# Seven products for the convolutions' half of an output projection, sums made on the output tiles, and an opening with its work put in another order

## The chip, the cores and the metric

The kernel runs on one core of a Trainium2 chip. A core has five engines with their own instruction queues: TensorE (PE, matmuls into PSUM), VectorE (DVE), ScalarE (ACT), GpSimd (POOL) and SyncE (SP), whose queue issues all the transfers here. The metric is the device time of one execution in microseconds, the median of several. All arithmetic is in float32. TensorE multiplies float32 operands in a form that keeps only the leading part of each (`fp32r`), so an operand is split into a high part (a copy on ScalarE that rounds) and a low part (a subtraction on VectorE), and a product is made of three matmuls: high by high, high by low, low by high.

## The reference

One decoder layer over a sequence of 2048 positions of 1024 features:

```python
h = rmsnorm(x, norm1_g)
p_q, p_k, p_v, p_g, p_a, c_b, c_c, c_h = split(h @ w_in)      # 256 256 512 512 16 512 512 512
o_gla = rmsnorm(gla(q, k, v, log_a)) * silu(p_g)              # gated linear attention, 4 heads of 128
o_conv = c_b * causal_depthwise_conv(c_c * c_h, conv_w)       # width 3 over positions, 512 features
x = x + concatenate([o_gla, o_conv]) @ w_out                  # 512 + 512 features -> 1024
h2 = rmsnorm(x, norm2_g)
x = x + (silu(h2 @ w_ffn_gate) * (h2 @ w_ffn_up)) @ w_ffn_down    # 1024 -> 2816 -> 1024
return rmsnorm(x, norm_f_g)
```

## The kernel before

Activations lie with features on the 128 partitions and positions along the free dimension: a tile is 128 features by 512 positions. The 2048 positions are four blocks of 512 and two halves of two blocks each. A half goes through a stage as one matrix of two block columns.

Most products are made with Strassen's scheme in Winograd's form, in *units*: a unit takes a weight matrix as four quarters (A11, A12, A21, A22) and an operand as four quarters (rows of features by the two blocks: B11, B12, B21, B22), and makes the 2 x 2 output tiles in seven products instead of eight. The list `PRODUCTS` pairs the weights A11, S1, S2, A12, S3, S4, A22 with the operands B11, T1, T2, B21, T3, B22, T4. The S are sums and differences of weight quarters, made on GpSimd in `unit_weights`; the T are differences of operand quarters (T1 = B12 - B11, T2 = B22 - T1, T3 = B22 - B12, T4 = B21 - T2), also made on GpSimd. Every weight quarter and every operand is split (lines 154 and 155, ScalarE and VectorE); `product_step` makes the three matmuls of a step (lines 399 to 401). `unit` lets products gather in two PSUM banks, and takes intermediate results out of them by a copy on ScalarE (line 419) and sums on VectorE (line 423). A product that adds to a bank has to wait until what was in it is read.

The stages follow one another on TensorE:

- *The opening.* `first_loads` and `build_h` load the first half's rows and tiles and norm them; `build_first` makes the first unit with eight products while the operands are being made, and its `differences` makes T1 to T4 in place, 16 subtractions on GpSimd (line 343) and 16 splits. The second unit (`plain_unit`) needs no T, so it has eight products too. The splits of the gate's weights (`gate_weights`) and the second half's statistics (`row_stats`) are background steps here.
- *The input projection* of each half, 12 units (`in_proj`); the results go to scratch tensors in device memory. The convolutions' features are multiplied out, split, and stored in both parts (`s_mix`). The linear attention (`gla_half`) is a background generator: steps of it are taken between products (`tick`).
- *The output projection* of each half (`out_proj`, lines 820 to 855), with plain products: for each pair of output tiles `d0`, all 8 tiles of features, 2 output tiles and 2 blocks, in four banks, 96 matmuls (lines 827, 828, 830). At its end x is added, on VectorE (line 852). In the second half's projection the first half's operands of the up projection are made beside it (`h2_first`, `h2_rest`); those named in `LATER` go through scratch first.
- *The up projection* of each half (`ffn_up`), 22 units; each pair of units gives four tiles of activations, of which seven kinds of operands are made, split (`split_later`), and stored in both parts (`s_act`).
- *The down projection* of each half (`ffn_down`): the 11 pairs of feature tiles are taken in groups of 2, 3, 3 and 3. For each group, all seven kinds of operands are loaded (`act_op`), and four units make the pairs of output tiles. The first group writes its results onto the output tiles `y`; the later groups add theirs to them, mostly on GpSimd (line 1000), after `unit` has put them together in tiles of its own.

What an engine does in which order is settled when the program is built: a scheduler with a model of the engines' times orders each queue, and `issue_after` holds an instruction behind another in that order. Pools of buffers set when loads can start: 28 operand tiles (`opp`), 2 raw weight tiles, 4 split weight tiles (`wqp`), 9 working tiles.

Of the kernel before, what the change touches and what calls it, by code (L numbers as in the profile page):

```python
# [19 lines left out]
P = 128  # L20
# [21 lines left out]
LATER = ("B21", "T3", "B22", "T4")  # L42
# [10 lines left out]
def tile_hymba_block(ctx, tc, x, xt, win, wa, wgu, wout, wffn, wdown, wdown_first, small, out):  # L53
# [48 lines left out]
    def scratch(name, n):  # L102
# [3 lines left out]

    s_kq, s_d, s_v, s_g = scratch("sk", 4), scratch("sd", 2), scratch("sv", 4), scratch("sg", 4)
    s_x1 = scratch("sx", KD)
    s_mix = [[dram.tile([P, 2, PB], F32, name=f"sm{b}_{k}") for k in range(4)] for b in range(NB)]
# [4 lines left out]
                n: dram.tile([P, 2, PB], F32, name=f"sa{half}_{m}_{n}")  # L114
# [7 lines left out]

    def made_ahead(name, n):
        return dram.tile([P, PB] if n in WHOLE else [P, 2, PB], F32, name=name)
# [26 lines left out]
    last_hi, raw_loads = [], []  # L151

    def split(src, hi, lo):
        last_hi[:] = [act.activation(hi, src, AF.Copy)]  # L154
        return dve.tensor_tensor(lo, src, hi.bitcast(F32), ALU.subtract)  # L155
# [150 lines left out]
    def build_first(quad, w):  # L306
# [29 lines left out]
        def differences(wanted):  # L336
            for n, y, a, b in (
# [10 lines left out]
    def plain_unit(src, ops):  # L348
# [3 lines left out]
        for r, row in enumerate(((0, 1), (3, 2))):  # L352
            w = [weight_quarter(raw[:, i, :]) for i in row]
            for j in range(2):
                o = bank()
                for i, n in enumerate(columns[j]):
                    for k in range(4):
                        product_step(o, w[i], ops[n], k, i == 0)
# [3 lines left out]

    def weight_quarter(src):
        n = src.shape[-1]
        h = wqp.tile([P, 2, PB], F32R, name="wq", tag="wq")[:, :, 0:n]
# [10 lines left out]
    def unit_weights(src):  # L376
        raw = raw_weights(src)
# [13 lines left out]
        w["A22"] = weight_quarter(a22)  # L391
        return w
# [10 lines left out]
    def unit(src, ops, into=None):  # L403


        w = unit_weights(src)
# [9 lines left out]

        def copied(name, o, at):
            t = tt(name) if into is None else into[at]
            act.activation(t[:], o[:], AF.Copy)  # L419
            return t  # L420

        def plus(t, o):
            dve.tensor_tensor(t[:], o[:], t[:], ALU.add)  # L423
            return t
# [14 lines left out]
        if into is not None:  # L439
# [20 lines left out]
    def row_stats(b):  # L460
        ssq = mtiny.tile([P, PT, 2], F32, name="ssq", tag="ssq")

        def fetch(t):
            xs = [bt("xn") for _ in range(2)]
            for e, xn in enumerate(xs):
                r0 = b * PB + t * P
                load(xn[:], x[r0 : r0 + P, e * PB : (e + 1) * PB])
# [4 lines left out]
        for t in range(PT):  # L472
# [5 lines left out]
            yield  # L478
# [48 lines left out]
    def gate_weights():  # L527
# [8 lines left out]
        split(r0, top[:, :, 2, :], top[:, :, 3, :])  # L536
        split(r0, top[:, :, 4, :], top[:, :, 5, :])
        split(r1, low[:, :, 2, :], low[:, :, 3, :])
# [90 lines left out]
    def in_proj(half, ops, first=None, differences=None):  # L629
        def units():  # L630
            for u in range(12):
                with ExitStack() as stack:
# [4 lines left out]
                    else:  # L637
                        us = plain_unit(win[u], ops) if u else first
# [6 lines left out]
        if half == 0:  # L645
            differences(("T1", "T2", "T3"))
# [7 lines left out]
        for i0 in (0, 2):  # L654
# [139 lines left out]
    def plain_weights(src, n):  # L794

        raw = rawp.tile([P, 4, PB], F32, name="raw", tag="raw")
        load(raw[:, 0:n, :], src)
        for i in range(n):
            h = weight_quarter(raw[:, i, :])
            for k in range(4):  # L800
                yield h[:, 0, k * P : (k + 1) * P], h[:, 1, k * P : (k + 1) * P]

# [8 lines left out]
    def build_mix(half):  # L811
        def pair(b, k):
            return load_pair(s_gla[b][:, k] if k < HEADS else s_mix[b][k - HEADS])

        return [[pair(2 * half + j, k) for j in range(2)] for k in range(KD)]
# [406 lines left out]
```

## Time and profile before

| | us |
|---|---|
| median of three runs | 2104.45 |
| lowest and highest | 2103.83, 2107.36 |
| the profiled execution, own time | 2106.52 |
| its span on the core | 2104.4 |
| TensorE busy | 2036.8 |
| VectorE busy | 1415.8 |
| ScalarE busy | 998.6 |
| GpSimd busy | 973.1 |

The profile is of one execution. A row of a group gives the line of the kernel, engine, operation, tile written and tiles read, shapes and count, then the busy time, the mean of one in ns, and the engine's idle time ahead of them with what ended most of it. A row in order of time gives start and duration in us, and in brackets the idle time before it and the instruction that ended it. Matmuls overlap, so their durations add up to more than the time that they take; the step from one start to the next is what one costs.

### The profile page before, as it was taken

What the parts mean: (1) busy time and instruction counts of PE and PEld (TensorE: products, weight loads), DVE (VectorE), ACT (ScalarE), POOL (GpSimd) and SP (SyncE); (2) the same over time, 40 slices, a digit from 0 to 9 for tenths busy, and PEclk for the clock granted to TensorE, in tenths of its full rate; (3) what the DMA queues carried; (4) which work ended last, traced back from release to release, by engine and by line L of the source; (5) the groups of instructions that cost most, each with busy time, mean ns of one, the idle gap of its engine ahead of it and who ended that gap; (6) DMA issues with size and microseconds to landing.
All of it is one profiled execution on the core that took longest, in us unless ns stands there. A gap on an engine that the chain in (4) does not pass through costs nothing.

```text
span 2104.4 us, 27023 instructions
## 1 busy us (share of the span) xinstructions
PE 2036.8 (97%) x9193; PEld 1656.3 (79%) x9193; DVE 1415.8 (67%) x2018; ACT 998.6 (47%) x1982; POOL 973.1 (46%) x704
## 2 busy tenths in 40 slices
PE   6999999999999999999999999999999999999996
PEld 4768888877888878788888878787888878877775
DVE  7669786549743786787786665557766677575554
ACT  6555455656542355445444443334544544443343
POOL 3436222222102564464464448865545544437773
PEclk9999999999999999999999999999999999999998
DMA  7349385425686862655545687695554544687672
GB/s 279 127 169 315 130 339 160 147 80 175 201 282 242 316 245 106 232 193 212 212 166 191 260 327 269 235 338 225 188 199 169 200 173 169 221 341 261 240 277 98
DMA packets 189241, 458.14 MB, mean 218 GB/s; under 512 B 19824, under 2 KB 65072, under 8 KB 179504
## 3 DMA queue, kind: packets, MB, share of 16 engines
q1 hardware_dynamic: 189104, 456.43, 60.1%
q8 instruction: 72, 1.18, 0.2%
q14 instruction: 65, 0.53, 0.1%
HBM read 294.34 MB, written 162.00 MB: 217 GB/s over the span
## 4 chain that ended last, share of the span: by engine, by line
PE 72%; DVE 7%; DMA 6%; issue 3%; ACT 2%; POOL 2%; SPq 1%; DVEq 0%; ACTq 0%; POOLq 0%
PE mm L399 20%; PE mm L401 20%; PE mm L400 20%; PE mm L827 3%; PE mm L828 2%; PE mm L830 2%; DVE wq L155 2%; DVE so L155 1%; DMA raw<-in_wdown_dram 1%; DMA op<-sa_T 1%; DMA x<-sx 1%; POOL y L1000 1%; ACT wq L154 1%; DMA sa_T<-so 1%; PE o_ps L751 1%
## 5 line engine op out<-in xcount | busy, mean ns | idle before, releaser
L399 PE MATMUL mm<-op,wq 128*128 128x512 f32 x2499 | 980.7, 394 | 20.1 <-ACT wq L154 8.4
L400 PE MATMUL mm<-op,wq 128*128 128x512 f32 x2499 | 975.8, 391 | 0.7 <-DVE op L155 0.7
L401 PE MATMUL mm<-op,wq 128*128 128x512 f32 x2499 | 965.5, 392 | 10.7 <-DVE wq L155 10.0
L155 DVE TENSOR_TENSOR wq<-raw,wq 128x512 fp32r<-128x512 f32 (+2 forms) x626 | 526.5, 848 | 335.8 <-ACT wq L154 333.4
L154 ACT ACTIVATE wq<-raw 128x512 fp32r<-128x512 f32 (+2 forms) x626 | 363.3, 587 | 551.5 <-PE mm L401 389.8
L399 PEld LDWEIGHTS mm<-op,wq 128*128 128x128 f32 x2499 | 470.8, 188 | 133.9 <-ACT wq L154 14.4
L401 PEld LDWEIGHTS mm<-op,wq 128*128 128x128 f32 x2499 | 470.5, 188 | 119.4 <-DVE wq L155 20.8
L400 PEld LDWEIGHTS mm<-op,wq 128*128 128x128 f32 x2499 | 470.9, 188 | 97.5 <-DVE op L155 1.3
L384 POOL TENSOR_TENSOR raw<-s,raw 128x512 f32<-128x512 f32 (+2 forms) x97 | 127.8, 1318 | 419.2 <-DVE wq L155 398.9
L423 DVE TENSOR_TENSOR c<-mm,c 128x512 f32<-128x512 f32 x267 | 183.0, 685 | 93.2 <-PE mm L401 91.1
L382 POOL TENSOR_TENSOR s<-raw 128x512 f32<-128x512 f32 (+2 forms) x97 | 129.1, 1331 | 212.0 <-DMA raw<-in_wffn_dram 88.0
L389 POOL TENSOR_TENSOR raw<-raw 128x512 f32<-128x512 f32 (+2 forms) x97 | 124.7, 1286 | 126.5 <-DVE wq L155 119.2
L419 ACT ACTIVATE c<-mm 128x512 f32<-128x512 f32 x267 | 154.7, 585 | 36.0 <-PE mm L401 34.5
L809 POOL TENSOR_TENSOR ssx<-ssx,q 128x512 f32<-128x512 f32 x52 | 76.2, 1477 | 154.4 <-ACT q L808 154.3
L383 POOL TENSOR_TENSOR raw<-raw 128x512 f32<-128x512 f32 (+2 forms) x97 | 136.7, 1409 | 4.1
L1000 POOL TENSOR_TENSOR y<-c,y 128x512 f32<-128x512 f32 x66 | 98.9, 1501 | 58.2 <-DVE c L423 56.3
L155 DVE TENSOR_TENSOR so<-t,so 128x512 fp32r<-128x512 f32 x96 | 93.2, 976 | 24.3 <-ACT so L154 24.2
L154 ACT ACTIVATE wq<-s 128x512 fp32r<-128x512 f32 (+2 forms) x97 | 56.8, 585 | 97.4 <-PE mm L401 85.0
L827 PE MATMUL mm<-op,wq 128*128 128x512 f32 x256 | 100.9, 395 | 0.0
L828 PE MATMUL mm<-op,wq 128*128 128x512 f32 x256 | 99.7, 389 | 0.0
L155 DVE TENSOR_TENSOR wq<-s,wq 128x512 fp32r<-128x512 f32 (+2 forms) x97 | 79.9, 823 | 15.1 <-ACT wq L154 14.5
L830 PE MATMUL mm<-op,wq 128*128 128x512 f32 x256 | 79.8, 390 | 0.0
(185 smaller groups left out, 1871.8 us busy)
## 6 DMA issues: line engine op xcount, KB each, us to landing
raw<-in_wffn_dram SPq DMA_DIRECT2D x44, 1024.0 KB, 6.4
sa_T<-so SPq DMA_DIRECT2D x88, 512.0 KB, 5.9
op<-sa_T SPq DMA_DIRECT2D x88, 512.0 KB, 9.5
sa_B<-so SPq DMA_DIRECT2D x69, 512.0 KB, 3.4
op<-sa_B SPq DMA_DIRECT2D x69, 512.0 KB, 9.2
raw<-in_win_dram SPq DMA_DIRECT2D x23, 1024.0 KB, 5.4
raw<-in_wdown_dram SPq DMA_DIRECT2D x24, 768.0 KB, 6.1
sx<-y SPq DMA_DIRECT2D x48, 256.0 KB, 3.1
```

Source lines behind the costliest of these rows:

```text
L154: last_hi[:] = [act.activation(hi, src, AF.Copy)]
L155: return dve.tensor_tensor(lo, src, hi.bitcast(F32), ALU.subtract)
L382: pool.tensor_tensor(s1, a21, a22, ALU.add)
L383: pool.tensor_tensor(a21, a11, a21, ALU.subtract)
L384: pool.tensor_tensor(a11, s1, a11, ALU.subtract)
L399: pe.matmul(o[:], wh, xh, start=first and k == 0, stop=False, skip_group_check=True)
L400: pe.matmul(o[:], wh, xl, start=False, stop=False, skip_group_check=True)
L401: return pe.matmul(o[:], wl, xh, start=False, stop=k == n - 1, skip_group_check=True)
L419: act.activation(t[:], o[:], AF.Copy)
L423: dve.tensor_tensor(t[:], o[:], t[:], ALU.add)
L827: pe.matmul(o[e, j][:], wh, m[:, 0, :], start=k == 0, stop=False)
L828: pe.matmul(o[e, j][:], wh, m[:, 1, :], start=False, stop=False)
```

## The change

- The output projection makes the convolutions' half in seven products. `seven_kinds` makes the seven kinds of operands from the four quadrants when the input projection is done with them, and stores them whole, without a split (`s_conv`); `build_mix` loads and splits them. The weights' part for the convolutions is taken as quarters of 2 x 128 columns with sums and differences on GpSimd; the heads' part stays plain. The sums go onto the tiles that hold x, nine additions in place of four, and the loads of x come one step earlier.
- `unit` can add its results onto given tiles (`onto`): the first read of a bank, a copy on ScalarE before, is then an addition on VectorE onto the output tile. The later groups of the down projection use it, and GpSimd's additions there go. A group's first raw weights are loaded ahead of its operands.
- The kinds named in `WHOLE` (T3, B22, T4) of the up projection's results are stored whole and split when they are loaded, like those of the other stages before. `LATER` takes in T1 and T2, and `h2_rest` loads straight into operand tiles.
- In the opening, the second unit's four weight quarters are split first; the differences, the gate's weights and the loads for the row statistics are ordered behind them.
- Two quarters of half width share one split weight tile (`weight_parts`).

```diff
-LATER = ("B21", "T3", "B22", "T4")
+LATER = ("T1", "T2", "B21", "T3", "B22", "T4")
...
 def build_first / differences
                 for k in range(4 if n in wanted else 0):
                     yy, aa, bb = [h[k + dk, j] for dk, j in (y, a, b)]
-                    pool.tensor_tensor(yy[:], aa[:], bb[:], ALU.subtract)
-                    ops[n].append(split_op(yy[:]))
+                    with tc.issue_after(los[-1].ins):
+                        pool.tensor_tensor(yy[:], aa[:], bb[:], ALU.subtract)
+                    with tc.issue_after(second_weights[0].ins):
+                        ops[n].append(split_op(yy[:]))
...
-    def plain_unit(src, ops):
+    def plain_unit(src, ops, differences):
...
-        for r, row in enumerate(((0, 1), (3, 2))):
-            w = [weight_quarter(raw[:, i, :]) for i in row]
+        w = [weight_quarter(raw[:, i, :]) for i in (0, 1, 3, 2)]
+        second_weights[:] = last_lo
+        differences(("T1", "T2", "T3"))
+        for r in range(2):
...
     def copied(name, o, at):
+            if onto is not None:
+                return plus(onto[at], o)
             t = tt(name) if into is None else into[at]
             act.activation(t[:], o[:], AF.Copy)
...
 def row_stats (and likewise the three splits of gate_weights)
-                load(xn[:], x[r0 : r0 + P, e * PB : (e + 1) * PB])
+                with tc.issue_after(second_weights[0].ins):
+                    load(xn[:], x[r0 : r0 + P, e * PB : (e + 1) * PB])
...
 def in_proj
-                hi = tp.tile([P, PB], F32R, name="hi", tag="t")
-                split(y[:], hi[:], y[:].bitcast(F32R))
-                dst = s_mix[2 * half + j][i0 + r]
-                store(dst[:, 0, :], hi[:].bitcast(F32))
-                store(dst[:, 1, :], y[:])
+            quadrants = [cc[r, j] for r in range(2) for j in range(2)]
+            seven_kinds(s_conv[half][i0 // 2], *quadrants)
...
 def out_proj, one pair of output tiles; mul: 2 steps of a product, plain: 4 steps for the heads
+            oa, ob, oc, od, oe = [None] * 5
+            w = tiles_quarter(a11)
+            pool.tensor_tensor(s1, a21, a22, ALU.add)
+            pool.tensor_tensor(a21, a11, a21, ALU.subtract)
+            pool.tensor_tensor(a11, s1, a11, ALU.subtract)
+            ws1 = tiles_quarter(s1)
+            oa = bank()
+            mul(oa, w, "B11", True)
+            add((0, 0), oa)
+            ob = bank()
+            mul(ob, ws1, "T1", True)
+            add((1, 1), ob)
+            w = tiles_quarter(v[:, 0:4, 1, :])
+            ws2 = tiles_quarter(a11)
+            oc = bank()
+            plain(oc, w, 1, True)
+            add((1, 1), oc)
+            od = bank()
+            plain(od, w, 0, True)
+            add((1, 0), od)
+            wa12 = tiles_quarter(a12)
+            pool.tensor_tensor(a12, a12, a11, ALU.subtract)
+            w = tiles_quarter(v[:, 0:4, 0, :])
+            mul(oa, ws2, "T2")
+            add((0, 1), oa)
+            oe = bank()
+            ws3 = tiles_quarter(a21)
+            mul(oe, wa12, "B21", True)
+            plain(oe, w, 0)
+            add((0, 0), oe, True)
+            mul(oa, ws3, "T3")
+            add((1, 1), oa, True)
...
+            plain(ob, w, 1)
+            mul(ob, ws4, "B22")
+            add((0, 1), ob, True)
+            mul(oa, wa22, "T4")
+            add((1, 0), oa, True)
...
 def h2_rest
-                ops[n].append(split_op(h[:]))
+                ops[n].append(load_whole(s_h2[n][k]))
...
 def split_later
+            if n in WHOLE:
+                store(dst[n][:], y[:])
...
 def ffn_down
+            if u:
+                raw = raw_weights(wdown[4 * u - 4])
+                with tc.issue_after(raw_loads[-1].ins):
+                    ops = {n: [group_op(m, n) for m in ms] for _, n in PRODUCTS}
...
-                for r, j, c, p in unit(src, ops):
-                    yy = y[d0 + r, j]
-                    eng = dve if p or last and half and r != j else pool
-                    eng.tensor_tensor(yy, c[:], yy, ALU.add)
+                onto = {(r, j): y[d0 + r, j] for r in range(2) for j in range(2)}
+                unit(src, ops, onto=onto, raw=None if d0 else raw)
...
-            gate_weights(), pause(9), row_stats(2), row_stats(3), gate(0, ops), unhurried(),
+            gate_weights(), pause(6), row_stats(2), row_stats(3), gate(0, ops), unhurried(),
```

More of the change, by code (lines that the diff above doesn't have):

```diff
@@ L401, in product_step, with unit @@
         return pe.matmul(o[:], wl, xh, start=False, stop=k == n - 1, skip_group_check=True)
-    def unit(src, ops, into=None):
-        w = unit_weights(src)
+    def unit(src, ops, into=None, onto=None, raw=None):
+        w = unit_weights(src, raw)
         def mul(i, o=None):
@@ L438, in unit @@
         mul(6, oa)
-        if into is not None:
+        if into is not None or onto is not None:
             copied("c21", oa, (1, 0))
@@ L637, in units @@
                     else:
[L638 removed]
+                        us = plain_unit(win[u], ops, differences) if u else first
                 if half == 0 and u == 1:
@@ new lines, in build_mix, with kinds, tiles_quarter @@
+        ops = {}
+        def kinds(*names):
+            for n in names:
+                ops[n] = [load_whole(s[n]) for s in s_conv[half]]
+        kinds("B11", "T1")
+        for j in (1, 0):
+            ops[j] = [load_pair(s_gla[2 * half + j][:, k]) for k in range(HEADS)]
+        kinds("T2", "B21", "T3", "B22", "T4")
+        return ops
+    def tiles_quarter(src):
+        n = src.shape[1]
+        h = weight_parts(n * P)
+        hi, lo = [h[:, e, :].rearrange("p (k c) -> p k c", c=P) for e in range(2)]
+        split(src, hi, lo)
+        return h
```

194 lines of the change are left out of this document (106 added, 88 removed).

## The prediction

> **What bounds the kernel now.** I read the page first, then TensorE's waits, then the stretches in which the change acts.
>
> ```profile
> span 2104.4 us, 27023 instructions
> PE 2036.8 (97%) x9193; PEld 1656.3 (79%) x9193; DVE 1415.8 (67%) x2018; ACT 998.6 (47%) x1982; POOL 973.1 (46%) x704
> PE   6999999999999999999999999999999999999996
> ```
>
> The kernel is bound by matmuls: TensorE (PE) is busy in 97% of the span, in all slices but the first and last. So only two things change the time: the number of matmuls, and the some 60 us in which TensorE waits.
>
> ```profile
> 2049.61 0.39 PE L400 MATMUL mm<-op,wq 128*128 128x512 f32 x1
> ...
> 2053.92 0.39 PE L401 MATMUL mm<-op,wq 128*128 128x512 f32 x1
> PE rb_ps L491 <- DVE rep L490: 13.9, 2, 13.7
> PE mm L401 <- DVE wq L155: 10.0, 7, 2.5
> PE mm L399 <- ACT wq L154: 8.4, 7, 1.7
> PE mm L399 <- ACT c L419: 7.0, 6, 2.6
> PE mm L399 <- DVE c L423: 2.5, 2, 1.9
> PE mm L399 <- DVE y L423: 1.6, 2, 0.8
> ```
>
> The first two rows (order of time) are the ends of a run of 20 matmuls without a wait: 4.31 us over 19 steps, 0.227 us each. That step, not the 0.39 us of one pipelined matmul, is the price of a matmul here. The others are the waits of TensorE: who waited for whom, us in all, times, longest. 13.9 us are the start, which the change leaves alone. The rest are weights that were split late (`wq`), and results that were not yet out of PSUM when the same bank was written again (`c`, `y`).
>
> **The change, part by part.**
>
> *A. The products.* In an output projection, one pair of output tiles (`d0`) took 96 matmuls (8 tiles of features, 2 output tiles, 2 blocks of positions, 3 matmuls each). Now the heads take 48 as before, and the convolutions' half takes 7 products of 2 tiles of 3 matmuls, 42. So 6 fewer in each of 8 pairs: 48 x 0.227 = **-10.9 us**. Nothing covers these matmuls, so the whole of it counts unless something new makes TensorE wait.
>
> *B. The opening.* Rows of TensorE in order of time, with the wait in brackets; then two windows (busy time by engine, granted clock, DMA share), a row of VectorE, and a group of its splits.
>
> ```profile
> 32.62 0.73 PE L330 MATMUL mm<-op,wq 128*128 128x512 f32 x2 [1.50 <-ACT op L154]
> 33.95 0.50 PE L331 MATMUL mm<-op,wq 128*128 128x512 f32 x1 [0.60 <-DVE op L155]
> 39.96 0.50 PE L331 MATMUL mm<-op,wq 128*128 128x512 f32 x1 [1.40 <-DVE op L155]
> 60.50 0.50 PE L399 MATMUL mm<-op,wq 128*128 128x512 f32 x1 [1.17 <-ACT wq L154]
> 63.76 0.50 PE L401 MATMUL mm<-op,wq 128*128 128x512 f32 x1 [2.06 <-DVE wq L155]
> 17.40:45.00 27.60, 23.84 (x87) 17.92 (x88) 24.55 (x40) 16.90 (x38) 11.43 (x8) 0.94 0.82 297
> 44.00:70.00 26.00, 22.76 (x91) 17.77 (x90) 25.76 (x29) 20.29 (x52) 18.29 (x13) 0.93 0.56 193
> 36.18 3.12 DVE L155 TENSOR_TENSOR wa_sb<-wa,wa_sb 128x64 fp32r<-128x64 f32 x3
> L155 DVE TENSOR_TENSOR op<-h,op 128x512 fp32r<-128x512 f32 x52 | 49.1, 981 | 3.4 <-ACT op L154 3.1
> ```
>
> VectorE (DVE) is full from 44 to 70 us (25.76 of 26.00), and the splits of the gate's weights alone hold it 3.12 us while TensorE needs an operand. The change puts the differences on GpSimd (POOL) behind the last split of `build_first`, and the differences' splits, the gate's weights and the row loads behind the second unit's four weight splits. The waits of 0.60, 1.40, 1.17 and 2.06 us should go (5.2 us); the 1.50 us stays, since it is the turn-round of the second block's norm, which does not move. The clock lost 6% of 27.6 and 7% of 26.0 us, 1.7 and 1.8 us; I count one of the two as saved. So -6.9 us.
>
> The work is moved, not removed, and what is late next is the first seven-product unit. It starts two units of 96 matmuls after 17.4 us and the first wait, near 65 us, and needs its third weight (`S2`) two products later, near 70.7. In the program's order on VectorE, 21 large splits now stand between the second unit's last weight and that one. They start near 46 us. At what a split cost in the old order (0.98 us in the group `op<-h`) they are done near 67, with the waits for GpSimd's 16 differences and nine small statistics among them near 74; without those they would be in time. I take 3 us of wait there and 1 us for transposes of the later row statistics, which TensorE reaches in line. **B: -3 us**, between -8.7 (all waits and both clock losses gone) and +1.
>
> ```profile
> L1000 POOL TENSOR_TENSOR y<-c,y 128x512 f32<-128x512 f32 x66 | 98.9, 1501 | 58.2 <-DVE c L423 56.3
> L423 DVE TENSOR_TENSOR c<-mm,c 128x512 f32<-128x512 f32 x267 | 183.0, 685 | 93.2 <-PE mm L401 91.1
> L419 ACT ACTIVATE c<-mm 128x512 f32<-128x512 f32 x267 | 154.7, 585 | 36.0 <-PE mm L401 34.5
> ```
>
> *C. The down projection's sums onto the output tiles.* For 23 units the 3 copies on ScalarE (585 ns) and 3 adds on GpSimd (1501 ns) leave, and 3 adds on VectorE (685 ns) come: 66 GpSimd adds, 98.9 us, go; VectorE gets 66 x 0.685 = 45 us. A unit is 63 matmuls, 14.3 us; VectorE then has 7 adds (4.8 us), 7 weight splits and about 2 of the splits in D; even at the 0.98 us of the crowded splits quoted above these are 8.8 us, 13.6 in all, so it still fits, with little to spare. In two places a unit's next product now waits for VectorE to read the bank rather than ScalarE; ScalarE cost 7.0 us there in the whole kernel, VectorE in its places 2.5 + 1.6. Four waits of this stage (the first two after GpSimd or a late load of weights):
>
> ```profile
> 1929.73 0.50 PE L399 MATMUL mm<-op,wq 128*128 128x512 f32 x1 [1.75 <-ACT wq L154]
> 1965.44 0.51 PE L399 MATMUL mm<-op,wq 128*128 128x512 f32 x1 [1.50 <-ACT wq L154]
> 2039.73 0.50 PE L399 MATMUL mm<-op,wq 128*128 128x512 f32 x1 [2.59 <-ACT c L419]
> 2054.87 0.50 PE L399 MATMUL mm<-op,wq 128*128 128x512 f32 x1 [0.56 <-ACT c L419]
> 1954.00:2010.00 56.00, 54.18 (x229) 43.50 (x228) 30.63 (x38) 18.74 (x37) 41.69 (x33) 0.97 0.61 232
> 1964.86 0.52 ACT L154 ACTIVATE wq<-raw 128x384 fp32r<-128x384 f32 x1 [2.97 <-DMA raw<-in_wdown_dram]
> 1928.13 0.99 POOL L384 TENSOR_TENSOR raw<-s,raw 128x384 f32<-128x384 f32 x1
> ```
>
> The wait at 1929.73 ends after GpSimd's weight difference at 1928.13, which stood behind its adds; that at 1965.44 ends after a weight load, which SyncE's queue now issues ahead of the group's operands. The two `c` waits have no copy any more. Together 6.4 us, and 3% of 56 us of clock, 1.7. **C: -8 us.**
>
> *D. T3, B22 and T4 stored whole.* In the up projection 66 splits leave both engines; in the down projection 66 splits come back behind the loads, on a load that is half as large (256 instead of 512 KB).
>
> ```profile
> op<-sa_T SPq DMA_DIRECT2D x88, 512.0 KB, 9.5
> ```
>
> A group's T4 is loaded when the last product of the group before is done and used 6 products, 12.2 us, later; 9.5 us of load and two splits on two engines are 11 us. It is close, and a late landing holds VectorE, with the sums and weights behind it in its queue. Six group starts: I take **+3 us** (0 to +9). In the up projection lighter queues shorten some of the `wq` waits: **-1 us** (-5 to +2). Stores of whole tiles now stand in SyncE's queue until GpSimd's last difference; a weight load behind one is late by some us of the 19 us that its unit has, so that costs nothing.
>
> *E. The second output projection.* All of its other new work meets the making of the up projection's operands.
>
> ```profile
> 688.00:775.50 87.50, 87.50 (x384) 71.77 (x383) 74.49 (x77) 34.42 (x60) 54.31 (x35) 1.00 0.85 306
> 730.03 1.74 POOL L300 TENSOR_TENSOR t<-h,t 128x512 f32<-128x512 f32 x1
> 730.54 1.77 DVE L155 TENSOR_TENSOR op<-t,op 128x512 fp32r<-128x512 f32 x1
> 732.24 0.68 DVE L155 TENSOR_TENSOR wq<-raw,wq 128x512 fp32r<-128x512 f32 x1
> 714.04 1.30 POOL L287 TENSOR_TENSOR t<-h 128x512 f32<-128x512 f32 x1 [0.63 <-DVE h L523]
> 753.07 2.47 DVE L852 TENSOR_TENSOR y<-y,mm 128x512 f32<-128x512 f32 x4
> L384 POOL TENSOR_TENSOR raw<-s,raw 128x256 f32<-128x256 f32 x8 | 6.0, 751 | 36.3 <-DVE wq L155 36.3
> L155 DVE TENSOR_TENSOR wq<-s,wq 128x256 fp32r<-128x256 f32 x8 | 3.6, 445 | 0.0
> ```
>
> VectorE is busy 74.5 of these 87.5 us, and TensorE nevertheless never waits. A split that meets a GpSimd instruction takes 1.77 us, one that does not 0.68 (0.60 to the next); the sums from PSUM take 0.62 each whatever GpSimd does. In each of the four pairs come 5 more sums (9 for 4), and 7 splits of 256 columns and 2 of 512 for 4 of 512, together 3.1 + 1.3 us, and 4 small differences on GpSimd (0.75 us). That is 17.6 us more for VectorE, and 12 us more of GpSimd to collide with, in a half that is 5.5 us shorter. Some 9 us were idle at its start; splits that come late are still ahead of their use, the last by 6 products, 16 us. What is late next are T1's to T4's splits of the first up unit, and with them its weights. Between 0 (all hidden) and +17 (all shown) I take **+7 us**, nearer the first bound's side since TensorE had no wait at 74.5 of 87.5. Beside the first output projection no such operands are made: 0.
>
> The Trainium skill, SBUF — State Buffer, "Who interferes with whom", says that a VectorE instruction with two SBUF inputs and a GpSimd instruction that reads SBUF exclude each other wholly, and that one with a single SBUF input does not contend. The second half agrees with the sums (0.62 us). By the first half a colliding pair would need 0.60 + 1.30 = 1.90 us where the rows give 1.77; the rival below works the stretch out so.
>
> *Sum.* -10.9 - 3 - 8 + 3 - 1 + 7 = **-12.9 us**. The profiled execution took 2106.52 us (span 2104.4), so its like would take 2093.6; it lay 2.1 us above the median of the three runs, so for the median 2104.45 - 12.9 = **2091.5 us**.
>
> **Rivals.**
> 1. *The covers hold and the waits go.* B at -8.7, D and E at 0: 2104.45 - 10.9 - 8.7 - 8 - 5 = 2072 at the end; some of it, 2076 to 2084. For it: the matmul stage E ran without a wait at a full VectorE. Against: so many small waits at 97% busy never vanished together.
> 2. *VectorE and GpSimd exclude each other strictly in E.* That is the page's rule, as a mechanism here. Of the 77 VectorE instructions of the window, 62 have two SBUF inputs (0.60) beside 35 of GpSimd (1.30), 82.7 us of 87.5; now 5.3 + 12 more, 100 us, in 81.7 us of matmuls, or 16 more to the last use. Without the late uses 18 us show: E +18 and B 0 give 2104.45 - 10.9 - 8 + 3 - 1 + 15 = 2102.5. For it: the 1.77 us rows. Against: the pair is 7% below exclusion, and much of GpSimd's work (sums of squares) has no hurry.
> 3. *Slower: VectorE waits in line for landings.* The last six kinds of operands of the up projection are loaded straight into operand buffers that the last pair frees one kind after another, where 11 spare buffers took four loads ahead before. Each kind whose landing is not covered holds VectorE's queue for a load, with the sums and weights behind it:
>
> ```profile
> h<-sfT SPq DMA_DIRECT2D x8, 256.0 KB, 7.8
> ```
>
> From three of six on it decides: 2091.5 - 7 + 23.4 = 2108; all six give 2131. Against: buffers come free 8 us or more ahead of each use.
>
> **How the numbers follow.** What a measurement can tell from no change is 0.2%, 4.2 us: faster is below 2100.2, slower above 2108.7. Forecast 0.53 (2084 to 2099), rival 1 0.13, rival 2 0.18 (half of it faster by over 0.2%), rival 3 0.16 (a fifth of it within 0.2%). Faster 0.53 + 0.13 + 0.07 = 0.73, same 0.09 + 0.04 = 0.13, slower 0.14. The range takes part of rivals 1 and 2 and the near end of 3: 2079 to 2108.
>
> **What would show it.** A right: 48 fewer matmuls of 512 columns at 0.227 us, an output projection near 82 us. B right: no waits of TensorE at 33 to 64 us, a wait of some us for `wq` near 70. C and D right: no GpSimd adds onto `y`, no `c` waits in the down stages, waits for `op` or `y` under 2 us at the groups' starts. E right: some waits for `wq` or `op` between the second output projection and the second up unit. I am wrong if those, or the opening's first seven-product unit, wait over 15 us together, or if sums on VectorE hold the bank in most down units.

## The result, and the profile after

The changed kernel takes 2112.6 us (median of 12 runs, 2108.9 to 2116.6) against 2105.7 us before (12 runs): ratio 1.0024, interval 1.0012 to 1.0035. It was forecast 13 us faster and is 5 to 7 us slower. The profiled execution took 2110.6 us, its span 2108.9.

The page of the changed kernel (span; busy time, share and instructions of each engine; TensorE's busy tenths in 40 slices), and the longest of its waits (who waited for whom: us in all, times, longest):

```profile
span 2108.9 us, 27139 instructions
PE 2027.9 (96%) x9145; PEld 1653.5 (78%) x9145; DVE 1487.9 (71%) x2176; ACT 977.5 (46%) x1960; POOL 931.5 (44%) x686
PE   6999999999989989999999999999999999999997
```

```profile
PE rb_ps L519 <- DVE rep L518: 14.2, 2, 14.0
PE mm L422 <- DVE y L902: 12.7, 6, 7.9
PE mm L424 <- DVE wq L162: 11.4, 11, 2.6
PE mm L422 <- ACT c L449: 6.9, 4, 3.7
...
PE mm L422 <- ACT wq L161: 5.4, 3, 3.6
PE sc L765 <- issue: 4.0, 1, 4.0
...
PE mm L422 <- DVE y L442: 2.6, 4, 1.7
```

The 48 instructions fewer on TensorE are there (9145 for 9193). The tenths have two dents that were not there before, in the 12th and 15th slice: the two output projections. The first row is the start, as before. The largest wait after it is a new one: TensorE waits for the sums of line 902, `out_proj`'s sums onto `y`. The waits for `y` in the down projection (line 442) come to 2.6 us and are the only ones of that kind there.

Where the time went is read by counting matmuls. The products' matmuls (tiles `mm<-op,wq`) are as many in both kernels in every stage but the output projections: 2040 before the first of these, 384 in each (360 with seven products), then 96 and 1752 in the first up projection, 924, 1848 and 933. So the starts of the n-th matmul in the two traces can be set against each other, stage by stage. The numbers are the us by which a stage is longer (+) or shorter (-) than before, the last row to the last of these matmuls. The input projections and the first output projection stand in one row, because 14 small matmuls of the attention lie before the border between them in the changed kernel and behind it in the kernel before. The experiments that follow have their columns here too (*neither* is without the squares' additions and without the partial sums). Two executions of one kernel differ by up to 5 us in the first row, by less than 1 us in the second, and by up to 4 us in the others.

| stage | changed | plain | seven_ first | seven_ second | no_ squares | no_ partials | neither | first_ paced |
|---|---|---|---|---|---|---|---|---|
| start to the end of the first output projection | +2.0 | -0.2 | +6.6 | -0.8 | +0.1 | +0.8 | +0.6 | -4.8 |
| second output projection | +14.0 | 0.0 | 0.0 | +11.6 | +2.3 | -0.7 | -3.8 | 0.0 |
| the next 96 matmuls (first up unit) | +5.0 | +2.1 | +0.5 | +4.2 | +3.5 | +4.5 | -1.0 | +6.8 |
| rest of the first up projection | -3.7 | -3.7 | -4.4 | -3.7 | -3.7 | -4.4 | -3.7 | -3.0 |
| first down projection | -0.7 | -2.2 | -0.9 | -3.5 | -3.0 | -1.1 | +0.5 | -2.2 |
| second up projection | -0.9 | -0.7 | +0.6 | -1.6 | -1.6 | +0.4 | +0.3 | -2.6 |
| second down projection | -11.3 | -12.9 | -11.2 | -13.5 | -12.0 | -10.8 | -11.0 | -12.4 |

So the down projection gained more than forecast, and the first three rows lost 21 us. (The expectation of *plain* below has 2.4, 13.6 and 5.0 for them, from borders set less closely.) The windows of the two output projections in the changed kernel (busy us of PE, PEld, DVE, ACT, POOL with instructions; granted clock; DMA share; GB/s):

```profile
585.60:689.10 103.50, 95.97 (x472) 78.86 (x470) 69.46 (x124) 46.52 (x119) 35.11 (x33) 0.98 0.80 266
689.10:791.50 102.40, 88.55 (x364) 70.29 (x363) 91.96 (x117) 37.50 (x76) 57.30 (x44) 0.93 0.78 262
```

In the second, VectorE has 91.96 us of work in 102.4 us, where 360 matmuls at 0.227 us need 82, and the clock was 0.93. TensorE's waits in that stage are these:

```profile
PE mm L422 <- DVE y L902: 8.9, 2, 7.9
PE mm L424 <- DVE wq L162: 3.7, 3, 2.0
PE tot L180 <- POOL ssx L838: 1.3, 1, 1.3
```

They are 13.9 us of the 19.4 that the stage is longer than 24 matmuls less would make it (14.0 and 5.4). The longest wait, and what stood on VectorE and GpSimd before it, each engine in order of time:

```profile
745.24 0.74 DVE L551 SCALAR_TENSOR_TENSOR h<-h,sml,rb 128x512 f32<-128x512 f32 x1
745.91 3.56 DVE L162 TENSOR_TENSOR wq<-raw,wq 128x256 fp32r<-128x256 f32 x3
749.39 2.92 DVE L551 SCALAR_TENSOR_TENSOR h<-h,sml,rb 128x512 f32<-128x512 f32 x2
752.23 0.67 DVE L902 TENSOR_TENSOR y<-y,mm 128x512 f32<-128x512 f32 x1
752.83 1.16 DVE L162 TENSOR_TENSOR op<-op 128x512 fp32r<-128x512 f32 x1
753.92 4.28 DVE L162 TENSOR_TENSOR wq<-raw,wq 128x256 fp32r<-128x256 f32 x3
758.12 1.74 DVE L162 TENSOR_TENSOR op<-op 128x512 fp32r<-128x512 f32 x1
759.79 0.68 DVE L902 TENSOR_TENSOR y<-y,mm 128x512 f32<-128x512 f32 x1
753.41 3.11 POOL L838 TENSOR_TENSOR ssx<-ssx,q 128x512 f32<-128x512 f32 x2
756.48 1.44 POOL L308 TENSOR_TENSOR t<-h,t 128x512 f32<-128x512 f32 x1
757.88 1.44 POOL L299 TENSOR_TENSOR t<-h,t 128x512 f32<-128x512 f32 x1
763.93 0.43 DVE L162 TENSOR_TENSOR wq<-raw,wq 128x256 fp32r<-128x256 f32 x1 [1.68 <-ACT wq L161]
760.52 0.80 PE L422 MATMUL mm<-op,wq 128*128 128x512 f32 x1 [7.93 <-DVE y L902]
762.39 0.63 PE L423 MATMUL mm<-op,wq 128*128 128x512 f32 x1
...
764.52 0.63 PE L422 MATMUL mm<-op,wq 128*128 128x512 f32 x1
```

In these rows VectorE runs without a gap up to the sums, and so does GpSimd up to 759.3. From the stage's start to 762 us VectorE has no idle time over 0.3 us, so it does not wait for GpSimd's results there. A weight split of 256 columns takes 1.2 to 1.4 us there on average (3.56 and 4.28 for three) and 0.43 at 763.93, where GpSimd had nothing to do. The sum at 759.79 stands behind all of it, and TensorE, whose next product needs a bank that such a sum has to read first, waits 7.93 us. The matmuls after it are 0.426 us apart (five steps from 762.39 to 764.52), nearly twice the 0.227 us: the clock stood at half.

### The profile page after: what moved, and what is told of

It is laid out like the page before. It is cut to its first block, busy times and chain, and to the rows that moved or that the text cites. A ratio compares the mean times of both kernels' runs of the same rounds, so it can differ in the third digit from the quotient of the medians.

```text
span 2108.9 us, 27139 instructions
## 1 busy us (share of the span) xinstructions
PE 2027.9 (96%) x9145; PEld 1653.5 (78%) x9145; DVE 1487.9 (71%) x2176; ACT 977.5 (46%) x1960; POOL 931.5 (44%) x686
## 4 chain that ended last, share of the span: by engine, by line
PE 80%; DVE 8%; DMA 5%; issue 3%; ACT 2%; POOL 1%; SPq 0%; DVEq 0%; ACTq 0%; POOLq 0%
PE mm L422 25%; PE mm L424 25%; PE mm L423 25%; DVE op L162 2%; DVE wq L162 2%; DMA op<-sa_T 1%; DVE h L551 1%; PE a_ps L620 1%; DMA op<-sc_T 1%; PE o_ps L789 1%; PE o_ps L791 1%; ACT wq L161 1%; ACT op L161 1%; DVE y L902 0%; DVE y L442 0%
## 5 line engine op out<-in xcount | busy, mean ns | idle before, releaser
L161 ACT ACTIVATE wq<-raw 128x512 fp32r<-128x512 f32 (+2 forms) x658 | 372.8, 574 | 606.4 <-PE mm L424 507.6
L422 PEld LDWEIGHTS mm<-op,wq 128*128 128x128 f32 x2739 | 517.0, 189 | 150.3 <-DVE y L902 15.1
L424 PEld LDWEIGHTS mm<-op,wq 128*128 128x128 f32 x2739 | 516.9, 189 | 126.6 <-DVE wq L162 17.2
L423 PEld LDWEIGHTS mm<-op,wq 128*128 128x128 f32 x2739 | 517.3, 189 | 109.5 <-DVE op L162 3.1
L442 DVE TENSOR_TENSOR c<-mm,c 128x512 f32<-128x512 f32 x198 | 135.7, 686 | 83.9 <-PE mm L424 82.1
L442 DVE TENSOR_TENSOR y<-mm,y 128x512 f32<-128x512 f32 x185 | 126.8, 687 | 80.3 <-PE mm L424 79.9
L162 DVE TENSOR_TENSOR op<-op 128x512 fp32r<-128x512 f32 x142 | 121.8, 888 | 7.6 <-ACT op L161 7.5
L449 ACT ACTIVATE c<-mm 128x512 f32<-128x512 f32 x198 | 115.5, 586 | 10.0 <-PE mm L424 8.6
L161 ACT ACTIVATE wq<-s 128x512 fp32r<-128x512 f32 (+2 forms) x105 | 60.1, 572 | 87.5 <-PE mm L424 86.1
L161 ACT ACTIVATE op<-op 128x512 fp32r<-128x512 f32 x142 | 82.9, 620 | 14.5 <-DMA op<-sa_T 6.6
L162 DVE TENSOR_TENSOR wq<-s,wq 128x512 fp32r<-128x512 f32 (+2 forms) x105 | 86.8, 827 | 2.6 <-ACT wq L161 1.9
L1100 POOL TENSOR_TENSOR y<-x,y 128x512 f32<-128x512 f32 x32 | 51.6, 1612 | 46.0 <-DVE y L442 41.3
L1014 DVE TENSOR_TENSOR c<-c,c 128x512 f32<-128x512 f32 x66 | 71.2, 1079 | 0.0
```

The lines of the kernel that those rows point to most:

```text
L162: last_lo[:] = [dve.tensor_tensor(lo, src, hi.bitcast(F32), ALU.subtract)]
L422: pe.matmul(o[:], wh, xh, start=first and k == 0, stop=False, skip_group_check=True)
L423: pe.matmul(o[:], wh, xl, start=False, stop=False, skip_group_check=True)
L424: return pe.matmul(o[:], wl, xh, start=False, stop=k == n - 1, skip_group_check=True)
```

## The experiments

**Which part costs, which gains.** The kernel *plain* has both output projections in eight products again, with the second up-operands stored and loaded as before; the other edits stay. *seven_first* and *seven_second* have one half in seven.

```
-    ssq = out_proj(0, build_mix(0))
+    ssq = plain_proj(0, plain_mix(0))     # the functions of before
...
-    ssq = out_proj(1, build_mix(1), h2_first(ssq, h2), h2_rest(h2))
+    ssq = plain_proj(1, plain_mix(1), h2_first(ssq, h2), h2_rest(h2))
```

> Both output projections again in eight products, as before the change, with the convolutions' features and the second up-operands (the list LATER) stored and loaded as before; the opening, the sums onto the output tiles and the whole stores stay changed. Theory V (the seven products cost their time in VectorE's queue during the two output projections and the first up unit, where the trace of after falls back by 2.4, 13.6 and 5.0 us against the trace of before at equal counts of matmuls): 2112.6 - 21 = 2091.6 us, 2089 to 2095, ratio to before about 0.993. Rival R (the loss belongs to the other edits, or to a clock that would be lost anyway): 2100 us or more.

> Seven products in the output projection of the first two batches only; the second one as before the change. Theory V (VectorE has room beside the first, whose stage it filled to 40 of 101 us before): the 24 matmuls less are worth -5.4, the waits seen there in the trace of after took 7.9 back, so +2.4 on the run with none: 2094 us, 2090 to 2098. Rival R2 (each half pays the same): +10, 2102 us.

> Seven products in the output projection of the last two batches only. Theory V: all but 2.4 us of the loss stays, 2110 us, 2107 to 2113. Rival R2 (each half pays the same): 2102 us.

Measured: plain 2085.4 us, ratio 0.9893 (0.9879 to 0.9906), better than both kernels; seven_first 0.9923 (0.9910 to 0.9937), seven_second 0.9952 (0.9940 to 0.9965). The seven products cost 1.0024 - 0.9893, some 28 us, and without them the change gains 23 us. Theory V had the place right and understated the size. It had the halves right for the first (2092.6 us, 2094 expected) and not for the second (2098.1 us, where it expected 2107 to 2113, and its rival 2102). The halves alone cost 6 and 12 us (0.9923 and 0.9952 less 0.9893), together 9 us less than both at once. A repetition of the changed kernel on another chip shows that this is no accident of one measurement:

> The changed kernel once more, to see whether seven products in both halves cost more than the sum of one half each (0.0033 + 0.0062 over the kernel with none): 1.0024 if the interplay of 8 us is real, 0.9985 if it was a difference between chips.

Measured: 1.0021 (1.0012 to 1.0030). Why both at once cost more stays open: in the first three rows of the table the traces give 19.1 us over plain for both and 5.1 and 13.1 for one half each, so only 1 of the 9 us lies there.

**What fills VectorE's queue.** Three edits of the changed kernel, in the two output projections alone: without GpSimd's additions of the squares, with these on VectorE, and without the five partial sums of a pair.

```
-            pool.tensor_tensor(ssq[:], ssq[:], q[:], ALU.add)     # no_squares
-            pool.tensor_tensor(ssq[:], ssq[:], q[:], ALU.add)     # squares_dve
+            dve.tensor_tensor(ssq[:], ssq[:], q[:], ALU.add)
...
-                dve.tensor_tensor(y[:], y[:], o[:], ALU.add)      # no_partials
                 if last:
+                    dve.tensor_tensor(y[:], y[:], o[:], ALU.add)
```

> The changed kernel without GpSimd's additions of the squares in the two output projections (28 instructions of 1.3 to 2 us; the sum of squares of the second norm is that of one tile alone, so the output is another one). Theory C (VectorE is late because GpSimd's instructions beside it slow its splits: 1.2 us for 256 columns where 0.41 are needed): VectorE gets some 14 x 1.1 x 0.65 = 10 us of the second half back, 2102 us, 2098 to 2107. Rival O (it is the order: a sum stands behind splits in VectorE's queue whatever GpSimd does): 2111 to 2113 us.

> The changed kernel without the five partial sums per pair of output tiles on VectorE in both output projections (40 sums of 0.68 us in the kernel; GpSimd's work is unchanged; the output is another one). Theory V (VectorE is over-full in the second output projection, whatever fills it): 20 x 0.68 = 13.6 us less in a stage that it filled to 92 of 102 us; the waits nearly go as they went without the squares, ratio 0.993 to 0.996. Theory G (GpSimd's own queue is what is late, VectorE only waits for it): no more than the waits for the sums, 12.7 us of TensorE, go, and waits for weights take their place: 0.999 to 1.002.

> The changed kernel with the additions of the squares in the two output projections on VectorE (0.69 us each) instead of on GpSimd (1.46 us). Theory C (GpSimd's instructions slow VectorE's splits): the collisions of 20 us of GpSimd's work go, 9.5 us of VectorE's work per half come; about half of what leaving them out gave (19 us), so 8 us below the changed kernel, ratio to before 0.9985, 0.996 to 1.000. Theory L (only the count of instructions on VectorE matters, GpSimd's neighbourhood costs nothing): 9.5 us more work in a full queue, 5 to 10 us above the changed kernel, 1.005 to 1.007.

> Control: the kernel with both output projections in eight products, also without GpSimd's additions of the squares there (the output is another one). Theory V (they cost time only where VectorE's queue is full): the same as with them, ratio 0.9893, within 0.002. Rival (they cost 19 us anywhere): 0.980.

Measured: no_squares 0.9936 (0.9924 to 0.9949), no_partials 0.9932 (0.9916 to 0.9948), squares_dve 0.9996 (0.9986 to 1.0005), plain_no_squares 0.9885 (0.9866 to 0.9904). Taking GpSimd's additions away gives 19 us, twice what theory C expected, and taking 20 sums a half from VectorE gives the same 19 us (this also takes away the banks' waits for these sums, which the first edit leaves in place). Where the queue has room, in plain, the same additions cost nothing that can be told. Moved onto VectorE they save some 6 us against the changed kernel where theory L expected a loss of 5 to 10: theory L falls. The second output projection without the squares:

```profile
687.30:778.00 90.70, 85.50 (x364) 68.96 (x363) 80.73 (x116) 37.19 (x76) 41.22 (x30) 0.98 0.88 296
L162 DVE TENSOR_TENSOR op<-op 128x512 fp32r<-128x512 f32 x18 | 13.4, 770 | 2.1 <-ACT op L161 2.0
```

In the changed kernel the same group reads:

```profile
L162 DVE TENSOR_TENSOR op<-op 128x512 fp32r<-128x512 f32 x19 | 19.4, 1037 | 0.6 <-ACT op L161 0.6
L838 POOL TENSOR_TENSOR ssx<-ssx,q 128x512 f32<-128x512 f32 x14 | 20.4, 1462 | 15.8 <-ACT q L837 15.8
```

VectorE's count of instructions is the same within one, and its busy time falls from 91.96 to 80.73 us: 20.4 us of additions on GpSimd held it for 11.2 us. The stage in *squares_dve* and in *no_partials*:

```profile
688.30:791.10 102.80, 90.77 (x366) 72.06 (x365) 91.18 (x132) 40.16 (x81) 42.15 (x30) 0.92 0.80 266
687.90:776.00 88.10, 85.53 (x365) 69.33 (x364) 83.56 (x95) 36.92 (x74) 61.88 (x45) 0.98 0.90 304
```

With the squares on VectorE it has 15 instructions more and is no longer busy (91.18 us): its own additions took the place of what GpSimd's cost it. The stage is as long as in the changed kernel, so the 6 us saved lie elsewhere; where is not shown. Without the partial sums GpSimd's work is all there, and the stage is 14.7 us shorter. So in this stage it is VectorE's time that decides, and GpSimd's work counts as part of it: 91 to 92 us of it went with 100 to 103 us of stage (seven_second has 91.8 in 100.4), 81 to 84 us with 88 to 91.

**Do seven products pay with room?** Both reliefs together:

> The changed kernel without both: GpSimd's additions of the squares and the five partial sums per pair of output tiles (another output). Theory V: with room on VectorE the 48 matmuls less show, 0.9888 (both output projections in eight products) less 10.9/2109: 0.9837, 0.982 to 0.986. Rival B (seven products wait for their banks or weights even with VectorE free): 0.988 or more.

Measured: 0.9894 (0.9881 to 0.9908), no better than plain; theory V expected 0.9837. But the table says where: the second output projection is now 3.8 us shorter than before, of the 5.4 of its 24 matmuls; theory V holds there. In the first three rows the trace is 6.2 us better than plain's; in the four later ones, where both kernels have the same code, it is 5.6 us worse, and why was not found. The first output projection keeps a wait of another kind, on an attention chunk:

```profile
623.10 1.23 PE L765 MATMUL sc<-kq 64*128 64x128 f32 x8 [4.12 <-DVE kq L755]
```

The background steps go by a count, `tick`; every second count issues a step of the chunks. Before the change the count went up every 12 matmuls, so a step came every 24 and not, as the expectation of *seven_first_paced* below has it, every 12. Now it goes up after each of a pair's eleven products, of which the four plain ones are 12 matmuls long and the seven others 6. *seven_first_dve* adds the first half's squares on VectorE; *paced* counts a product of 6 matmuls as half:

```
-            tick()
+            beat[0] += 1 if n == 2 else 0.5
+            if beat[0] >= 1:
+                beat[0] -= 1
+                tick()
```

> Seven products in the first output projection alone, its squares added on VectorE. Theory V: VectorE was busy 69 of 103 us there, the 13 additions (9 us) fit and the collisions go; 24 matmuls less, -5.4, against waits of 3 us: 0.987 to 0.989. Rival (the waits there are those of the attention chunks behind VectorE's queue, which grows): 0.991 to 0.994.

> Seven products in the first output projection alone, and the attention chunks beside it stepped once per 12 matmuls, as in eight products, where the changed kernel steps them after every product, of which the seven are 6 matmuls long. Theory P (the chunk's steps come too close for VectorE, and TensorE waits 3 to 4 us for `kq` and then runs at half clock): these go, 24 matmuls less show, 0.986 to 0.989 against 0.9888 to 0.9893 with eight. Rival (the pace does nothing, the first half costs what it cost): 0.992.

> The same with the squares of the first output projection added on VectorE. Theory P: 0.985 to 0.988, the fastest of all. Rival: 0.992.

Measured: seven_first_dve 0.9920 (0.9906 to 0.9933), seven_first_paced 0.9918 (0.9904 to 0.9931), both together 0.9930 (0.9916 to 0.9943). In time nothing is won: theory V's 0.987 to 0.989 and theory P's 0.985 to 0.989 are missed, and each time the rival had the number. In the trace of seven_first_paced the waits for `kq` and `y` of 0.7 to 2.8 us are gone (0.28 and 1.75 are left, the clock is 1.00), and the first row of the table is 4.8 us shorter than before. With the squares on VectorE as well the same row is only 1.2 us shorter, so that is within what two executions differ by. The first up unit, 100 us later, gives it back:

```profile
780.00 0.50 PE L424 MATMUL mm<-op,wq 128*128 128x512 f32 x1 [3.27 <-ACT wq L163]
784.20 0.80 PE L426 MATMUL mm<-op,wq 128*128 128x512 f32 x1 [3.37 <-DVE wq L164]
```

Plain has one wait of 2.18 us there, and the row is 6.8 us longer than before against plain's 2.1. The paced steps also move the points at which the later background work is issued; whether that makes these weights late was not tried.

**The other edits, one undone at a time, from plain.** The opening as before; the down projection's results copied by ScalarE and added by GpSimd; T3, B22 and T4 split before their store; a group's weights loaded behind its operands.

```
-        differences(("T1", "T2", "T3"))      # old_opening: called in in_proj, unordered,
-                with tc.issue_after(second_weights[0].ins):   # and no issue_after
...
-                unit(src, ops, onto=onto, raw=None if d0 else raw)     # copied_sums
+                for r, j, c, p in unit(src, ops, raw=None if d0 else raw):
+                    eng.tensor_tensor(yy, c[:], yy, ALU.add)
...
-            if n in WHOLE:                   # split_stores
-                store(dst[n][:], y[:])
...
-                raw = raw_weights(wdown[4 * u - 4])     # operands_first
```

> Both output projections in eight products, and the opening as before the change (gate weights, differences, row statistics). The opening's share by the traces at equal counts of matmuls is between +0 and +2 us: by that 0 to 2 us faster than with the drawn-out opening, ratio 0.988 to 0.9893. By the prediction's step B (-3 us) it would be slower, 0.9907.

> Both output projections in eight products and the opening as before, once more: 0.9911 if the drawn-out opening gains 3 to 4 us, 0.989 if the first comparison was a difference between chips (the traces show no gain in the opening).

> Both output projections in eight products, and the down projection's results copied by ScalarE and added by GpSimd as before the change (weights still loaded ahead of the operands, T3, B22 and T4 still stored whole). By step C most of the 8 us come back, ratio about 0.9925 against 0.9893. Rival D2 (the down projection gained by something else, the whole stores or the order of loads): within 2 us of the kernel with sums onto y, 0.989 to 0.990.

> Both output projections in eight products, and T3, B22 and T4 split before they are stored, as before the change. By step D (+3 at the groups' starts, -1 in the up projection) this is 2 us faster, ratio 0.9885. Rival D2 (the whole stores gain, by the 4.3 us by which the first up projection and up to 13 us by which the last down projection are shorter in the traces): 0.993 to 0.996.

> Both output projections in eight products, and a group's first weights loaded behind its operands, as before the change. By step C it brings back the wait of 1.50 us and the lost clock of 1.7 us at the start of one group, 3 us, ratio 0.9908. Rival D2 (this order is the main gain of the down projection): 0.993 or more; rival D3 (it does nothing): 0.9893.

> The kernel with both output projections in eight products once more, beside the three that undo one part each on the same chip: ratio 0.988 to 0.9905.

| kernel | median us | ratio to before (interval) | the edit's gain by this |
|---|---|---|---|
| plain, plain_again | 2085.4, 2086.3 | 0.9893 (0.9879 to 0.9906), 0.9888 (0.9873 to 0.9903) | |
| old opening, again | 2089.1, 2086.8 | 0.9911 (0.9895 to 0.9926), 0.9900 (0.9885 to 0.9915) | 2 to 4 us, not clear of noise |
| copied sums | 2098.0 | 0.9952 (0.9938 to 0.9965) | 12 us |
| split stores | 2091.7 | 0.9917 (0.9904 to 0.9929) | 5 us |
| operands first | 2084.2 | 0.9887 (0.9873 to 0.9901) | none |

The gains add up to some 20 of plain's 23 us. The second down projection before its last units, in the kernel with copied sums and in plain:

```profile
1864.00:2062.00 198.00, 192.39 (x833) 155.08 (x833) 141.23 (x179) 97.04 (x190) 138.71 (x107) 1.00 0.53 196
```

```profile
1864.80:2052.00 187.20, 186.53 (x816) 152.27 (x815) 137.78 (x208) 78.86 (x153) 91.36 (x74) 1.00 0.56 207
```

The second window has 17 matmuls less, 3.9 us of the 10.8 between them. With sums onto `y`, TensorE idles 0.7 us of 187 (5.6 of 198 with copies), and VectorE's busy time is no longer, although it has 29 instructions more: GpSimd's 138.7 us beside it are 91.4.

## Why the prediction was wrong

- **A (-10.9)** was right in count (48 matmuls less). Its time showed only where the cover was taken away, and not whole: -3.8 us in the second half without squares and partial sums, against -5.4. For the first half the traces with paced chunks (-4.8 and -1.2) do not settle it. "Nothing covers these matmuls" held; the condition behind it, "unless something new makes TensorE wait", is what came.
- **B (-3)** was near in sum (2 to 4 us by the times). In detail: the waits of 1.40, 1.17 and 2.06 us went, 0.60 stayed, and the third weight of the first seven-product unit came late as forecast, by 3.61 us for the 3 us taken, with 1.12 us on the next weight behind it:

```profile
77.69 0.50 PE L422 MATMUL mm<-op,wq 128*128 128x512 f32 x1 [3.61 <-ACT wq L161]
79.55 0.80 PE L424 MATMUL mm<-op,wq 128*128 128x512 f32 x1 [1.12 <-DVE wq L162]
```

```profile
67.54 8.06 DVE L162 TENSOR_TENSOR op<-h,op 128x512 fp32r<-128x512 f32 x6
```

Six of the differences' splits took 1.34 us each there, not 0.98. In the first row of the table the kernels with the new opening and with the old (plain -0.2 and -1.6, old opening -0.5 and +2.2) lie within what two executions differ by, so where the times' gain lies stays open.
- **C (-8)** was right in kind, short in size: 12 us for the sums alone. The order of loads, from which 3 of the 8 were expected, gave nothing.
- **D (+3 and -1)** had the wrong sign: a gain of 5 us. No late operand held VectorE at the groups' starts (waits for `op` and `wq` there of 0.2 to 0.7 us), and the first up projection gained 3.7 us behind its first unit; with the stores split that was 1.0. Fewer splits on a busy VectorE were priced at 1 us.
- **E (+7, 0 to +17)** is the step that failed. Its sum of VectorE's work was right: 74.5 + 17.6 = 92.1 us, measured 91.96. The conclusion was not. "nearer the first bound's side since TensorE had no wait at 74.5 of 87.5" took the room of the old stage as cover for the new work, though the new stage had only 82 us of matmuls for 92 us of work. That excess is 10 us, and the stage lost 14.0 + 5.4 = 19.4 us. The rest is VectorE's own idle time, 10.4 us of the 102.4. It does not lie at the stage's start, where the old kernel had its 9 us (VectorE is busy for the whole of the first 10.9 us now), but behind the longest wait:

```profile
760.00:776.00 16.00, 15.48 (x58) 12.66 (x59) 6.82 (x13) 3.81 (x8) 6.65 (x6) 0.84 0.51 186
```

9.1 us of it fall between 762 and 776 us. VectorE stands there for weight splits, whose first halves on ScalarE had waited for TensorE's matmuls, and for a product's end. So VectorE's full queue made TensorE wait, and TensorE's delay then left VectorE without work. What waited was also another thing than forecast: not only weights (3.7 us), but a bank, for a sum in VectorE's queue (8.9 us). The waits had a price that the step left out, the half clock: 13.7 us of the stage had it, 5.5 of them under the longest wait itself, and some 17 matmuls came 0.43 us apart, about 3.4 us more.
- **E, behind the stage.** 5.0 us more went into the first up unit (2.1 in plain). The longest wait there is for a copy on ScalarE, which stood behind a weight split; that had waited 3.77 us for a weight difference on GpSimd, and this stood behind an addition of squares:

```profile
798.41 4.00 POOL L838 TENSOR_TENSOR ssx<-ssx,q 128x512 f32<-128x512 f32 x1 [7.56 <-ACT q L837]
805.35 0.50 PE L422 MATMUL mm<-op,wq 128*128 128x512 f32 x1 [3.71 <-ACT c L449]
```

- **E, the 0 beside the first output projection,** was wrong as well. Seven products there alone cost 6 us by the times, in place of the 5.4 saved; in the changed kernel TensorE waited 4.0 us at an attention chunk and 3.5 us for sums of line 902. VectorE had room on the whole (69.5 of 103.5 us), but not at the attention chunks.
- The **rivals**: in mechanism the nearest was the second, GpSimd and VectorE in each other's way. Its sum has a slip: the text has E +18 and B 0, the sum +15; with the text's terms it gives 2105.5 and not 2102.5. The additions held VectorE for 11.2 of their 20.4 us. By the Trainium skill, "SBUF — State Buffer", "Who interferes with whom", from which its stricter form came, they could hold it for up to 20.4 (an estimate, if every addition met a VectorE instruction with two SBUF inputs); the trace agrees in direction and does not reach that bound. In number the third lay nearer (2108 and up), but not by its mechanism: an operand that landed late held ScalarE once, for 3.09 us at 790.30, and VectorE behind it for 0.64 us; in the 10 us after that TensorE waited 0.5 us for a weight and 0.3 for a sum. The chances have a slip too: half of 0.18 is 0.09 and a fifth of 0.16 is 0.03, so faster is 0.75, same 0.12, slower 0.13.

In sum: B, C and D gained about 20 us where 9 were forecast, and the seven products, forecast at -3.9 us (A and E), cost 28.

## What to carry to other kernels

Set an engine's new work against the new length of its stage: matmuls saved shorten the time in which everything else must fit, and here a supporting engine at 85% (74.5 of 87.5 us) turned that into a loss larger than the saving. Idle time that comes only behind a wait is no cover. Time on GpSimd beside VectorE's splits is to be counted into VectorE's sum, here at about half (11.2 of 20.4 us). When a change holds several edits, undo them one at a time: here four of them gained or were neutral and the named one lost more than all of them brought; the kernel without it is the fastest, at some 2085 us.

## What the runs showed that was not expected

TensorE can pay twice for a wait: after 7.93 us of waiting the matmuls came 0.426 us apart instead of 0.227. In stretches around that wait:

```profile
752.00:758.00 6.00, 0.58 (x3) 0.16 (x1) 6.00 (x6) 0.63 (x1) 6.00 (x5) 0.75 0.82 261
758.00:764.00 6.00, 3.48 (x8) 2.83 (x9) 4.32 (x7) 1.14 (x3) 2.60 (x2) 0.50 0.76 280
764.00:770.00 6.00, 6.00 (x25) 4.86 (x25) 3.27 (x6) 0.84 (x2) 2.13 (x2) 0.90 0.10 37
```

The granted clock is 0.50 in the second and comes back in the third; it had gone down during the wait. In the changed kernel waits of 2.04 us (at 717.3), 2.10 (129.1) and 2.55 (867.1) were also followed by 3.4 us at half clock; in the kernel before, the wait of 2.59 us at 2039.73 was not. What decides between them is not shown.

And 28 additions on GpSimd, 1.46 us each in the second half, for which TensorE itself waits once (1.3 us, the first matmul of the norm's sum), cost 19 us of run time in the changed kernel and nothing measurable in plain.
